# Issuing the first Strassen weight sums of w_bl and w_out one quad earlier in a hybrid decoder layer on Trainium2

## The chip, the core and the metric

The kernel runs on one core of one Trainium2 chip. The metric is device time in microseconds (us), as the median of several runs; the profile is that of one execution, taken by the hardware profiler. The engines go by these names: PE is TensorE's matmul, PEld its weight load, DVE is VectorE, ACT is ScalarE, POOL is GpSimd, and SP issues most of the DMAs. Each engine works through its own queue in order, and semaphores make it wait for the others.

## The reference

One layer on a sequence of 1024 tokens with 1024 channels, in float32. An RMS-normalised input goes through a large projection `w_in`. Its parts feed two branches. The S5 branch (a complex diagonal state-space model) ends in a gated linear unit with `w_glu` and the projection `w_bs`; the RG-LRU branch ends in `w_bl` (1280 x 1024). The two results are merged by gates and multiplied with `w_out` (1024 x 1024). Then come a residual sum and a gated per-layer embedding with `w_ple` and `w_ple_gate`:

```python
z_l = (y_l * jax.nn.silu(lru_g)) @ w_bl[i]
merged = jax.nn.sigmoid(gate_s) * z_s + jax.nn.sigmoid(gate_l) * z_l
x = x + rms_norm(merged @ w_out[i], g_post[i])
x = x + (p[i] @ w_ple[i]) * jax.nn.sigmoid(x @ w_ple_gate[i])
```

## The kernel before

**Arithmetic.** A float32 product is made of three faster ones. Each operand is split into a high part (a rounded copy, type fp32r) and a low part (the rest), and `three` (line 315) issues the matmuls high x high (L317), then high x low and low x high (both L319), each of a 128 x 128 weight block with 128 x 512 data. So the weight's low part is loaded last of the three.

**The weight stream.** `weight_plan` (line 37) lists all weights once, in the order in which PE uses them, as 212 "quads" of up to four blocks of 128 x 128, counted from 0. Class `Weights` walks this list. `load` (L163) issues the DMA of a chunk of eight blocks from HBM into one of four raw buffers; `fetch` decides in the program when a chunk may be loaded. `make` prepares quad after quad in a ring of six buffers: ACT writes the high part (L222). For plain quads of w_bs, w_out and most of w_ple_gate, ACT then writes the negated rounded value into the low part's place (L225), and a DMA that POOL issues adds the raw value to it (L226). For every other quad the low part is "owed", and `lows` has DVE subtract (L234) a little later. `next` hands a quad to the matmuls, and `ahead` is called ahead of each quad:

```python
    def ahead(self, held=1):
        n = self.pos + self.RING - 1 - held
        self.make(n)
        self.lows(n - 1)
        self.fetch(n + 8)
        self.sum(n + 2)
```

Here `pos` is the quad that PE's program uses next, so with `held` at 1 quad `pos + 4` is made and the sums reach to `pos + 6`.

**Strassen pairs.** Part of w_bl's and of w_out's product is done by Strassen's method, which saves one product in eight. Its weights are sums and differences of blocks. Two chunks, a pair, hold A11, A12 and A21, A22. The list then has quads of other kinds than "plain": O2 stands for S2 = A21 + A22 - A11, S1 for A21 + A22, S3 for A11 - A21, S4 and O4 for A12 - S2, A22 for itself. `sum` (line 179) issues these on POOL, one instruction each (all L194): at an O2 quad S1 and S2, in buffers that each pair uses again, and the others at their own quads. At an O2 quad it also calls `lows(i)` (line 204), which has DVE make all low parts owed up to there, since those of the pair before still read the buffers.

**The order around the change.** Quads 112 to 119 are plain quads of w_glu, used alternately by `ps_eb` and `ps_ea` in `brows` (line 1248; 24 matmuls a quad). Quads 120 to 143 are the four pairs of w_bl: O2, S1, a plain quad, S3, S4, A22 each. Quads 144 to 151 are plain quads of w_bs, whose products (`ps_F`) are gated into the merged rows `mg`. Quads 152 to 157 are plain quads of w_out, used in `product` (line 1495; 12 matmuls a quad): 152 to 155 start the banks `oX0` to `oX3`, 156 and 157 add to the first two. Then follow four pairs of w_out, quads 158 to 173, each O2, S3, S1 and S4 or O4, whose products go to `oY`, `oZ`, `oW` and `oV`. After each product `tick` (line 329) runs one step of the data-side work: beside 152 `t_raw(3)` (line 1388), where DVE makes differences of merged rows (L1390, L1391, L1393, L1395) that ACT and DVE split (`lagged`, L1367, and `flush`, L1374), and beside 153 the first of the T1 operand. ACT, DVE, POOL and PE are issued in the order written in the program (`manual_schedule`); SP's order is the scheduler's.

Of the kernel before, what the change touches and what calls it, by code (L numbers as in the profile page):

```python
# [116 lines left out]
BLOCKS, QUADS = weight_plan()  # L117
# [18 lines left out]
class Weights:  # L136
# [42 lines left out]
    def sum(self, upto):  # L179
        G = self.nc.gpsimd  # L180
        while len(self.ready) <= min(upto, len(QUADS) - 1):
            i = len(self.ready)
            self.fetch(i)
            q = QUADS[i]
            s = self.sums
            if q[0] == "O2" and len(self.done) < i:
                return

            def add(name, a, b, op, into=None):
                if into is None:  # L190
                    s[name] = self.tmp.tile([P, HT], F32, tag=name, name=f"w{name}_{i}")
                else:
                    s[name] = s[into]
                G.tensor_tensor(s[name], s[a], s[b], op)  # L194

            if q[0] == "plain":
                _, c, o, n = q
                self.ready.append((self.raws[c][:, o * P:(o + n) * P], n))
                continue
            if q[0] in FIRST:  # L200
                r0, r1 = (self.raws[c] for c in q[1:3])
                s.update(A11=r0[:, :HT], A12=r0[:, HT:], A21=r1[:, :HT], A22=r1[:, HT:])
            if q[0] == "O2":
                self.lows(i)
                add("S1", "A21", "A22", ALU.add)
                add("S2", "S1", "A11", ALU.subtract)
            if q[0] in ("S4", "O4"):
                add("S4", "A12", "S2", ALU.subtract, "S2")
            if q[0] == "S3":
                add("S3", "A11", "A21", ALU.subtract, "A21")  # L210
            self.ready.append((s[q[0].replace("O", "S")], 4))
# [41 lines left out]
def tile_hybrid_trunk(  # L253
# [43 lines left out]
    make_identity(nc, ident)  # L297
    halfpi = cst([P, 1], "halfpi", math.pi / 2)
    cp_t = cst([P, sum(n for _, n in CPAR)], "cp_t")
    sp8 = cst([P, NL], "sp8")  # L300
    nsp8 = cst([P, NL], "nsp8")
# [173 lines left out]
    ple_sb = [two_rows(i, f"ple_sb{i}") for i in (4, 5, 13, 2)]  # L475
    scratch = page(8, "scratch", F32)
    NPAR = sum(n for _, n in SPAR)
    NPT = NPAR - 2048
    pt = scratch[:, :NPT]
# [1218 lines left out]
```

## Time and profile before

| | |
|---|---|
| median of 3 runs | 928.76 us (928.12 to 930.4) |
| profiled execution | 928.25 us, its span 926.5 us |
| mean granted clock of TensorE | 0.999 |
| DMA | 134.21 MB, mean 145 GB/s |

The page of the profile gives for each engine its busy time, share of the span and number of instructions. A view of waits gives, for an engine, the instruction that waited, what released it, and then the total, the number of times and the longest. A timeline gives per row the start, the length, engine, line and operation, what is written from what, and in brackets the idle time before it with its releaser. Times count from the start of the span. `wq` is a quad in the ring, `wraw` a raw chunk, `wS` a sum, `mT` and `mB` operands of w_out's product.

### The profile page before, as it was taken

What the parts mean: (1) busy time and instruction counts of PE and PEld (TensorE: products, weight loads), DVE (VectorE), ACT (ScalarE), POOL (GpSimd) and SP (SyncE); (2) the same over time, 40 slices, a digit from 0 to 9 for tenths busy, and PEclk for the clock granted to TensorE, in tenths of its full rate; (3) what the DMA queues carried; (4) which work ended last, traced back from release to release, by engine and by line L of the source; (5) the groups of instructions that cost most, each with busy time, mean ns of one, the idle gap of its engine ahead of it and who ended that gap; (6) DMA issues with size and microseconds to landing.
All of it is one profiled execution on the core that took longest, in us unless ns stands there. A gap on an engine that the chain in (4) does not pass through costs nothing.

```text
span 926.5 us, 11716 instructions
## 1 busy us (share of the span) xinstructions
PE 919.0 (99%) x4228; PEld 760.3 (82%) x4228; DVE 624.6 (67%) x977; ACT 469.1 (51%) x714; POOL 150.6 (16%) x159
## 2 busy tenths in 40 slices
PE   9999999999999999999999999999999999999997
PEld 7888888888888888888888888888888887887886
DVE  6885566666664347766666767687862798886863
ACT  6643233444443356666666668544534355558531
POOL 1218112212220000000000000022322126422100
PEclk9999999999999999999999999999999999999999
DMA  9745445564533201111111116811479975499951
GB/s 358 277 126 160 126 142 166 172 171 133 173 97 113 74 29 52 52 46 51 52 52 52 47 34 216 291 56 55 141 255 244 247 193 206 119 245 233 301 184 56
DMA packets 70442, 134.21 MB, mean 145 GB/s; under 512 B 18416, under 2 KB 32880, under 8 KB 70384
## 3 DMA queue, kind: packets, MB, share of 16 engines
q1 hardware_dynamic: 64768, 122.72, 41.7%
q0 software_dynamic: 5472, 10.49, 6.3%
q8 instruction: 33, 0.54, 0.2%
q10 hardware_dynamic: 144, 0.26, 0.1%
q14 instruction: 25, 0.20, 0.1%
HBM read 95.30 MB, written 27.53 MB: 133 GB/s over the span
## 4 chain that ended last, share of the span: by engine, by line
PE 89%; issue 6%; DMA 2%; DVE 1%; POOL 1%; ACT 0%; POOLq 0%; SPq 0%
PE ps_L L319 16%; PE ps_L L317 8%; PE ps_rx L319 8%; PE ps_rg L319 8%; PE ps_rg L317 4%; PE ps_rx L317 4%; PE ps_F L319 3%; PE ps_u L319 3%; PE bZ L319 3%; PE ps_pg L319 2%; PE bW L319 2%; PE pg L319 2%; PE bX L319 2%; PE ps_ple L319 2%; PE ps_ea L319 2%
## 5 line engine op out<-in xcount | busy, mean ns | idle before, releaser
L319 PE MATMUL ps_L<-hB,wq 128*128 128x512 f32 x640 | 197.4, 390 | 0.0
L319 PEld LDWEIGHTS ps_L<-hB,wq 128*128 128x128 f32 x640 | 120.3, 188 | 24.3
L317 PE MATMUL ps_L<-hB,wq 128*128 128x512 f32 x320 | 127.1, 397 | 0.0
L222 ACT ACTIVATE wq<-wraw 128x512 fp32r<-128x512 f32 (+1 forms) x188 | 112.5, 613 | 24.1 <-issue 9.2
L234 DVE TENSOR_TENSOR wq<-wraw,wq 128x512 fp32r<-128x512 f32 (+1 forms) x152 | 105.0, 706 | 3.1 <-ACT wq L222 3.1
L319 PE MATMUL ps_rg<-hB,wq 128*128 128x512 f32 x320 | 98.5, 389 | 0.0
L319 PE MATMUL ps_rx<-hB,wq 128*128 128x512 f32 x320 | 98.5, 389 | 0.0
L319 PE MATMUL ps_pg<-x1hl,wq 128*128 128x512 f32 x240 | 74.9, 392 | 0.3 <-DVE x1hl L1374 0.2
L317 PEld LDWEIGHTS ps_L<-hB,wq 128*128 128x128 f32 x320 | 60.2, 188 | 13.3 <-issue 1.7
L319 PEld LDWEIGHTS ps_rg<-hB,wq 128*128 128x128 f32 x320 | 60.1, 188 | 12.5
L319 PEld LDWEIGHTS ps_rx<-hB,wq 128*128 128x128 f32 x320 | 60.1, 188 | 12.4
L194 POOL TENSOR_TENSOR wS<-wraw 128x512 f32<-128x512 f32 x8 | 12.4, 1549 | 354.8 <-DMA wraw<-w_blocks 343.3
L1078 DVE SCALAR_TENSOR_TENSOR c<-ps_rx,cp_t,c 128x1023 f32<-128x1023 f32 (+2 forms) x30 | 38.5, 1282 | 46.2 <-ACT c L1076 45.5
L317 PE MATMUL ps_rx<-hB,wq 128*128 128x512 f32 x160 | 62.3, 389 | 0.0
L317 PE MATMUL ps_rg<-hB,wq 128*128 128x512 f32 x160 | 62.3, 389 | 0.0
L319 PEld LDWEIGHTS ps_pg<-x1hl,wq 128*128 128x128 f32 x240 | 44.8, 188 | 11.5 <-DVE x1hl L1374 1.7
L1015 ACT ACTIVATE sg<-ps_L 128x1024 f32<-128x1024 f32 x20 | 20.5, 1027 | 59.7 <-issue 52.5
L226 POOL DMA_DIRECT2D wq<-wraw x36 | 31.8, 883 | 100.1 <-ACT wq L225 65.6
L317 PE MATMUL ps_pg<-x1hl,wq 128*128 128x512 f32 x120 | 47.0, 391 | 0.0
L319 PE MATMUL ps_u<-hB,wq 128*128 128x512 f32 x128 | 39.8, 392 | 0.4 <-DVE hB L736 0.4
L319 PE MATMUL ps_F<-ys,wq 128*128 128x512 f32 x128 | 39.4, 389 | 0.0
L1086 ACT ACT_TABLE_LOAD x9 | 11.5, 1283 | 51.2 <-DVE yr L1115 51.2
(360 smaller groups left out, 1927.0 us busy)
## 6 DMA issues: line engine op xcount, KB each, us to landing
wraw<-w_blocks SPq DMA_DIRECT2D x95, 512.0 KB
wq<-wraw POOLq DMA_DIRECT2D x36, 256.0 KB, 6.0
xt<-x_t SPq DMA_DIRECT2D x8, 512.0 KB
ple_d<-ple_sb SPq DMA_DIRECT2D x8, 512.0 KB
wn<-sbt SPq DMA_DIRECT2D x8, 512.0 KB
sgl_d<-sg SPq DMA_DIRECT2D x8, 512.0 KB
wn<-pt_d SPq DMA_DIRECT2D x16, 256.0 KB
sgs_d<-sg SPq DMA_DIRECT2D x8, 512.0 KB
```

The lines of the kernel that those rows point to most:

```text
L194: G.tensor_tensor(s[name], s[a], s[b], op)
L222: nc.scalar.activation(hi, src, AF.Copy)
L226: nc.gpsimd.dma_start(lo.bitcast(F32), src, accum_op=ALU.add)
L234: self.nc.vector.tensor_tensor(lo, src, hi.bitcast(F32), ALU.subtract)
L317: T.matmul(ps, wh, xh, start=start, stop=False, skip_group_check=more)
L319: T.matmul(ps, a, b, start=False, stop=stop and a is (wh if xl_last else wl), skip_group_check=more)
L1015: S.activation(t, ps, AF.Sigmoid)
L1078: V.scalar_tensor_tensor(c[:, d:], ps[:, :NT - d], w_[3 - d], c[:, d:], ALU.mult, ALU.add)
L1086: S.activation(sq, ps, AF.Sigmoid)
```

## The change

In `sum`, the test that holds back the sums of an O2 quad is replaced. Before, they waited until every quad ahead of it was made. Now they are held back only while their chunk's load has not been issued in the program, or while a quad that is not plain is still unmade ahead.

```diff
             q = QUADS[i]
             s = self.sums
-            if q[0] == "O2" and len(self.done) < i:
+            if q[0] == "O2" and (q[1] not in self.raws or any(QUADS[j][0] != "plain" for j in range(len(self.done), i))):
                 return
```

`self.done` is the list of made quads and `self.raws` holds the chunks whose loads were issued. What is summed, by which instructions and into which buffers stays as it was.

## The prediction

> **What bounds the kernel now.** I read the page's busy times first, then the waits of PE (the matmul engine) and of its weight loads.
>
> ```profile
> PE 919.0 (99%) x4228; PEld 760.3 (82%) x4228; DVE 624.6 (67%) x977; ACT 469.1 (51%) x714; POOL 150.6 (16%) x159
> ...
> PE warm L500 <- DVE halfpi L291: 1.1, 1, 1.1
> PE ps_ple L317 <- DVE p_hi L526: 0.8, 1, 0.8
> PE ps_u L319 <- DVE hB L736: 0.4, 1, 0.4
> PE oY L319 <- DVE wq L234: 0.3, 1, 0.3
> PE ps_pg L319 <- DVE x1hl L1374: 0.2, 1, 0.2
> ...
> PEld oY L319 <- DVE wq L234: 1.0, 2, 0.7
> ```
>
> PE is busy 919.0 of 926.5 us, and all its named waits come to 2.8 us. Only one has to do with Strassen weight sums: `oY`, the product that uses the O2 quad of w_out, waits for a low part. No product of w_bl is in either list. So little can be gained, and only in the w_out stage. The timeline of PE there, around that wait:
>
> ```profile
> 768.39 0.39 PE L317 MATMUL oY<-mT,wq 128*128 128x512 f32 x1
> ...
> 769.29 0.50 PE L319 MATMUL oY<-mT,wq 128*128 128x512 f32 x1 [0.29 <-DVE wq L234]
> ...
> 771.69 0.39 PE L317 MATMUL oZ<-mT,wq 128*128 128x512 f32 x1
> ...
> 774.41 0.39 PE L317 MATMUL oW<-mT,wq 128*128 128x512 f32 x1
> ```
>
> A quad is 12 matmuls. Undisturbed it takes 774.41 - 771.69 = 2.72 us; this one took 771.69 - 768.39 = 3.30. The wait costs **0.58 us**, and that is the largest gain there is.
>
> **What moves.** In the planned order quads 112 to 119 (w_glu) and 144 to 157 (w_bs, then plain w_out) are plain; O2 of the first pair is quad 120 for w_bl and 158 for w_out. The old test issues its sums when all earlier quads are made, in the call of `ahead` that makes quad 119 or 157. The new test lets them out in the call before, since `sum` looks two quads past the last one made and the one still unmade is plain. Later pairs have A22, S4 or O4 ahead of them, so their test comes out as before. No instruction is added; S1 and S2 move up one quad, and S3 stays where it is.
>
> POOL's timeline shows what its queue holds at the two places (L226 issues the DMA that completes a low part, L194 is a sum), and SP's one load before each:
>
> ```profile
> 603.96 1.30 POOL L194 TENSOR_TENSOR wS<-wraw 128x512 f32<-128x512 f32 x1 [335.77 <-DMA wraw<-w_blocks]
> ...
> 758.01 0.86 POOL L226 DMA_DIRECT2D wq<-wraw  x1 [6.32 <-ACT wq L225]
> 761.87 0.86 POOL L226 DMA_DIRECT2D wq<-wraw  x1 [3.00 <-ACT wq L225]
> 762.43 1.61 POOL L194 TENSOR_TENSOR wS<-wraw 128x512 f32<-128x512 f32 x1
> 764.12 1.63 POOL L194 TENSOR_TENSOR wS<-wS,wraw 128x512 f32<-128x512 f32 x1
> 765.71 1.74 POOL L194 TENSOR_TENSOR wraw<-wraw,wraw 128x512 f32<-128x512 f32 x1
> ...
> 597.25 0.43 SPq L163 DMA_DIRECT2D wraw<-w_blocks  x1
> ...
> 747.23 0.33 SPq L163 DMA_DIRECT2D wraw<-w_blocks  x1
> ```
>
> **The w_bl pair: nothing.** POOL stood idle for 335.77 us ahead of S1 and was released by a load's landing. Its queue was empty, so an earlier place in the program cannot start the sum earlier. What does change is DVE's order: `lows(i)` at line 204 now flushes the low part of quad 118 one call earlier, and no longer takes that of quad 119 with it, which goes out one call later.
>
> ```profile
> 609.55 0.67 DVE L234 TENSOR_TENSOR wq<-wraw,wq 128x512 fp32r<-128x512 f32 x1
> ...
> 614.72 1.29 DVE L234 TENSOR_TENSOR wq<-wraw,wq 128x512 fp32r<-128x512 f32 x2
> ...
> 632.39 0.39 PE L317 MATMUL ps_ea<-geo,wq 128*128 128x512 f32 x1
> ```
>
> At 609.55 is quad 117, at 614.72 are 118 and 119. One moves to 610.2 and delays what follows by 0.6 us; the other moves a quad of 24 matmuls, 5.4 us, to about 621. PE first needs quad 119 at 632.39, so 11 us cover it. Cost 0; if DVE were 11 us behind there, it would cost what exceeds that.
>
> **The w_out pair: sums ahead of the DMA of quad 157.** The queue was DMA(156), DMA(157), S1, S2, S3; it becomes DMA(156), S1, S2, DMA(157), S3. From a DMA's issue to the next sum POOL takes 762.43 - 761.87 = 0.56 us, so S1 can start at 758.01 + 0.56 = **758.57**. Its raw data were loaded from 747.23; the load at 597.25 took until 603.96, 6.7 us, so I put this landing at 753.9, in time. S1 and S2 take 765.71 - 762.43 = 3.28 us and end at 761.85, when DMA(157) went out before. In the queue alone nothing is lost. But DVE and ACT are not idle in those 3.3 us. ACT's timeline, then DVE's, then DVE's two instructions under the old sums as a group:
>
> ```profile
> 759.30 0.63 ACT L1367 ACTIVATE mT<-mtmp 128x512 fp32r<-128x512 f32 x1 [1.10 <-DVE mtmp L1391]
> 759.90 0.63 ACT L1367 ACTIVATE mT<-mg 128x512 fp32r<-128x512 f32 x1
> 760.44 0.61 ACT L222 ACTIVATE wq<-wraw 128x512 fp32r<-128x512 f32 x1
> 760.96 0.62 ACT L225 ACTIVATE wq<-wraw 128x512 fp32r<-128x512 f32 x1
> ...
> 761.96 1.14 ACT L1367 ACTIVATE mT<-mg 128x512 fp32r<-128x512 f32 x2
> ...
> 765.79 0.63 ACT L222 ACTIVATE wq<-wS 128x512 fp32r<-128x512 f32 x1 [2.69 <-POOL wS L194]
> ...
> 758.57 0.69 DVE L1391 TENSOR_TENSOR mtmp<-mg,mg 128x512 f32<-128x512 f32 x1
> 759.18 0.69 DVE L1393 TENSOR_TENSOR mg<-mg,mg 128x512 f32<-128x512 f32 x1
> ...
> 762.61 1.99 DVE L1374 TENSOR_TENSOR mT<-mg,mT 128x512 fp32r<-128x512 f32 x1 [0.75 <-ACT mT L1367]
> ...
> L1374 DVE TENSOR_TENSOR mT<-mg,mT 128x512 fp32r<-128x512 f32 x2 | 3.7, 1883 | 0.8 <-ACT mT L1367 0.8
> ```
>
> A DVE tensor_tensor takes 0.69 us alone and 1.88 (mean of two) while POOL sums. The moved sums fall on `t_raw(3)`: L1391 starts at 758.57, the very time S1 can start, and L1393 behind it. ACT's splits at 759.30 and 759.90 wait for these two, and behind them in ACT's queue stand both halves of quad 157 (760.44, 760.96), for whose end DMA(157) waits. So a stretch on DVE passes through ACT and POOL to the low part of quad 157. How late that may be, from PE's weight loads and from what the landing view gives for DMA(157) and for DMA(156):
>
> ```profile
> 765.45 0.19 PEld L317 LDWEIGHTS oX<-mB,wq 128*128 128x128 f32 x1
> 765.67 0.41 PEld L319 LDWEIGHTS oX<-mB,wq 128*128 128x128 f32 x2
> ...
> DMA to landing us min/median/max: 3.2/3.2/3.2
> ...
> DMA to landing us min/median/max: 3.7/3.7/3.7
> ```
>
> Quad 157 starts 2.72 us before 768.39, at 765.67; its first low part is the second of the two loads listed at 765.67, at about 765.90. The DMA landed at 761.87 + 3.2 = 765.07: slack 0.83, or 0.33 with the other landing time. Two ends for the stretch. If DVE gets L1391 in first, only L1393 is stretched, by 1.88 - 0.69 = 1.19 us: PE waits 1.19 - 0.83 = 0.36 to 1.19 - 0.33 = 0.86. If S1 is first, both are, by 1.99 - 0.69 + 1.19 = 2.49: PE waits 1.66 to 2.16. I take the first: DVE runs without a gap there and has L1391 at hand, while S1 still has to follow a DMA issue. Middle 0.61.
>
> In return S2 is done at about 762.4 instead of 765.75. ACT no longer stands 2.69 us before 765.79, and the low part of quad 158 is no longer late: even with quad 157 delayed, hi(158) follows the two T1 splits of 761.96, at 761.96 + 1.19 + 1.14 = 764.3. That gives back the 0.58. Next in line would be DVE's backlog, which PE's delay covers.
>
> On who waits, the Trainium skill, in "SBUF — State Buffer", section "Who interferes with whom", says that a DVE instruction with two SBUF inputs contends with a GpSimd instruction that reads SBUF, and that whoever issues first holds the shared ports for the whole instruction. The instruction at 762.61 agrees: it ended 0.56 us after S1 (762.43 + 1.61). By the group's mean both DVE instructions would be stretched whoever comes first, and PE would wait 2.38 - 0.83 = 1.55 to 2.38 - 0.33 = 2.05 us; by the rule the first of a tie goes free, which is the lower end I took.
>
> **The sum**, on the profiled execution (928.25 us, of which the span is 926.5): -0.58 + 0.61 = +0.03, so 928.28; bounds -0.58 + 0.36 = -0.22 to -0.58 + 2.16 = +1.58. The median of the runs, 928.76, is 0.51 above the profiled execution, so I add that: **928.8**.
>
> **Rivals.**
> - *Clean gain*: the sums slip into POOL's pause and DVE's stretch stays under the slack. For: POOL had 3.00 us idle before 761.87. Against: L1391 and L1393 lie exactly there. Gain 0.58: 928.2.
> - *POOL wins the tie*: both DVE instructions are stretched and PE waits about 1.9 at quad 157, net +1.33: 930.1. For: at 762.61 it was DVE that was held. It decides from the point where S1 starts before 758.57.
> - *The sum waits for its raw load* and holds DMA(157) behind it on POOL. Every us that the load lands after 758.57 passes to PE once the slack is gone: net = landing + 3.28 + 3.2 - 765.90 - 0.58 = landing - 760.0. To be slower by 0.3% (2.8 us) the landing must be after 762.8, 15.6 us from issue against 6.7, or the load issued 9 us later. SP's queue is ordered by the scheduler, not by hand, so I don't exclude it: 931.6 or more.
> - *Nothing moves*: S1 doesn't start earlier at w_out either, as at w_bl. 928.8 again. Against: POOL's releaser at 761.87 is ACT, not a load.
>
> **The numbers.** Forecast 0.42; POOL wins 0.23; clean gain 0.2; nothing moves 0.1; late load 0.05. A measurement of this kernel can tell about 0.3%, 2.8 us, from no change; all but the last stay inside. The runs before spread over 2.3 us, so the range is 928.2 and 930.1 with half that spread, 1.1, on either side: 927.1 to 931.2. Faster by more than 0.3% has no case, only scatter, 0.03; slower has the last case and scatter, 0.07; same 0.90.
>
> **What would show it.** S1 near 758.6 to 759.2 ahead of the last L226 on POOL; L1393 stretched to some 1.9 us; that last L226 at 763 or later and a wait of 0.4 to 0.9 us of `oX` on the DMA shortly after 765.7; `oY` with no wait on L234, its quad in 2.72 us; S1 of w_bl still released by a load at about 604. It is wrong if any stage but w_out changes by over 1 us, or if quad 157 loses nothing while `oY` still waits.

## The result, and the profile after

The changed kernel takes 929.22 us (median of 22 runs, 928.93 to 933.01) against 928.26 us (22 runs, 927.82 to 930.4): a ratio of 1.0013, 95% interval 1.0007 to 1.0019. By the interval that is 0.6 to 1.8 us slower (the medians lie 0.96 us apart), less than the 0.3% named in the prediction, and its interval lies clear of 1. The profiled execution took 929.39 us, its span 927.6 us, 1.1 more than before.

The page's busy times and the waits of PE and its weight loads, after:

```profile
PE 918.9 (99%) x4228; PEld 760.3 (82%) x4228; DVE 626.0 (67%) x977; ACT 469.1 (51%) x714; POOL 150.3 (16%) x159
...
PE oX L319 <- DMA wq<-wraw: 1.4, 1, 1.4
...
PEld oX L319 <- DMA wq<-wraw: 1.9, 1, 1.9
```

The wait of `oY` on L234 has left the list, and a larger one has come: `oX`, on the DMA that completes a low part. PE's timeline shows where, and what it costs:

```profile
765.78 0.39 PE L317 MATMUL oX<-mB,wq 128*128 128x512 f32 x1
766.01 0.39 PE L319 MATMUL oX<-mB,wq 128*128 128x512 f32 x1
767.83 0.50 PE L319 MATMUL oX<-mB,wq 128*128 128x512 f32 x1 [1.43 <-DMA wq<-wraw]
...
770.24 0.39 PE L317 MATMUL oY<-mT,wq 128*128 128x512 f32 x1
...
772.96 0.39 PE L317 MATMUL oZ<-mT,wq 128*128 128x512 f32 x1
```

Quad 157 now takes 770.24 - 765.78 = 4.46 us, 1.74 more than an undisturbed quad; the named wait is 1.43 of this. Quad 158 behind it takes 772.96 - 770.24 = 2.72: its 0.58 is won. The chain behind the loss, read upward from the DMA: POOL's timeline, then DVE's, then ACT's.

```profile
604.81 1.68 POOL L194 TENSOR_TENSOR wS<-wraw 128x512 f32<-128x512 f32 x1 [336.52 <-DMA wraw<-w_blocks]
...
758.13 0.86 POOL L226 DMA_DIRECT2D wq<-wraw  x1 [6.32 <-ACT wq L225]
758.69 1.61 POOL L194 TENSOR_TENSOR wS<-wraw 128x512 f32<-128x512 f32 x1
760.38 1.64 POOL L194 TENSOR_TENSOR wS<-wS,wraw 128x512 f32<-128x512 f32 x1
764.56 0.86 POOL L226 DMA_DIRECT2D wq<-wraw  x1 [2.55 <-ACT wq L225]
...
758.68 2.17 DVE L1391 TENSOR_TENSOR mtmp<-mg,mg 128x512 f32<-128x512 f32 x1
760.78 1.77 DVE L1393 TENSOR_TENSOR mg<-mg,mg 128x512 f32<-128x512 f32 x1
...
760.89 0.63 ACT L1367 ACTIVATE mT<-mtmp 128x512 fp32r<-128x512 f32 x1 [2.58 <-DVE mtmp L1391]
762.59 0.63 ACT L1367 ACTIVATE mT<-mg 128x512 fp32r<-128x512 f32 x1 [1.07 <-DVE mg L1393]
763.13 0.62 ACT L222 ACTIVATE wq<-wraw 128x512 fp32r<-128x512 f32 x1
763.65 0.62 ACT L225 ACTIVATE wq<-wraw 128x512 fp32r<-128x512 f32 x1
```

S1 starts 0.56 us behind the DMA issue at 758.13, and both DVE instructions of `t_raw(3)` are held, not one. L1391 ends at 760.85, 0.55 after S1 (760.30). ACT's splits wait for the two, the halves of quad 157 stand behind the splits, and the last DMA goes out at 764.56, 2.69 later than before (0.11 of this comes from an earlier stage). POOL was free from 762.02 and waited 2.55 us for ACT. At w_bl, the first row, S1 is still released by a load.

The span's 1.1 us adds up from PE's timelines: 0.11 us before the w_out products (these start at 752.18 instead of 752.07), 1.74 lost at quad 157, 0.58 won at 158, and 0.13 won at the `oY` of the second pair: 0.11 + 1.74 - 0.58 - 0.13 = 1.14.

### The profile page after: what moved, and what is told of

It is laid out like the page before. It is cut to its first block, busy times and chain, and to the rows that moved or that the text cites. A ratio compares the mean times of both kernels' runs of the same rounds, so it can differ in the third digit from the quotient of the medians.

```text
span 927.6 us, 11719 instructions
## 1 busy us (share of the span) xinstructions
PE 918.9 (99%) x4228; PEld 760.3 (82%) x4228; DVE 626.0 (67%) x977; ACT 469.1 (51%) x714; POOL 150.3 (16%) x159
## 4 chain that ended last, share of the span: by engine, by line
PE 88%; issue 6%; DVE 2%; DMA 2%; POOL 1%; ACT 0%; POOLq 0%; DVEq 0%; ACTq 0%
PE ps_L L319 16%; PE ps_L L317 8%; PE ps_rg L319 8%; PE ps_rx L319 8%; PE ps_rg L317 4%; PE ps_rx L317 4%; PE ps_u L319 3%; PE bZ L319 3%; PE ps_F L319 3%; PE ps_pg L319 2%; PE bW L319 2%; PE bX L319 2%; PE pg L319 2%; PE ps_ple L319 2%; PE ps_ea L319 2%
## 5 line engine op out<-in xcount | busy, mean ns | idle before, releaser
L234 DVE TENSOR_TENSOR wq<-wraw,wq 128x512 fp32r<-128x512 f32 (+1 forms) x152 | 105.2, 708 | 3.2 <-ACT wq L222 3.1
```

The costliest lines, as they stand in the source:

```text
L234: self.nc.vector.tensor_tensor(lo, src, hi.bitcast(F32), ALU.subtract)
```

## The experiments

All eight were timed in five rounds, 11 runs each against 33 of the kernel before on the same chip; a profile shows one of the 11. The stretch theory: the moved sums hold up DVE, DVE holds up ACT, and ACT the DMA of quad 157. The rivals: POOL's queue order by itself, or the work at w_bl. Line numbers shift with the lines that an experiment adds; the operations tell which is which.

**Which pair.** The test was changed for one pair at a time.

```diff
-            if q[0] == "O2" and len(self.done) < i:
+            if q[0] == "O2" and len(self.done) < i - (i == 158):    # wout_only
+            if q[0] == "O2" and len(self.done) < i - (i == 120):    # wbl_only
```

> The earlier issue for quad 158 (w_out) alone, w_bl's first pair as before. Stretch theory (the moved sums S1 and S2 stretch DVE's two instructions of t_raw(3), ACT's halves of quad 157 wait for those, and PE waits for that quad's low part): all of the loss is here, ratio 1.0011 to 1.0013, a wait of oX on a DMA of 1.4 us. Rival (the loss comes from DVE's changed order at w_bl or from SP's order that the scheduler changed): a ratio within 0.0005 of 1.

> The earlier issue for quad 120 (w_bl) alone, w_out's first pair as before. Stretch theory: POOL's first sum is released by its load as before, DVE's changed order is covered, ratio 1.0000 within 0.0004, oY's wait of 0.3 us is still there. Rival (the loss comes from w_bl): ratio 1.0010 or more.

`wout_only` gave 1.0011 (1.0003 to 1.002), `wbl_only` 0.9998 (0.9989 to 1.0007). From `wbl_only`: POOL's first sum, DVE's low parts of w_glu's last quads, and the old wait in PE's list.

```profile
604.03 1.30 POOL L194 TENSOR_TENSOR wS<-wraw 128x512 f32<-128x512 f32 x1 [336.07 <-DMA wraw<-w_blocks]
...
609.62 1.28 DVE L234 TENSOR_TENSOR wq<-wraw,wq 128x512 fp32r<-128x512 f32 x2
620.06 0.70 DVE L234 TENSOR_TENSOR wq<-wraw,wq 128x512 fp32r<-128x512 f32 x1
...
PE oY L319 <- DVE wq L234: 0.2, 1, 0.2
```

Low part 118 has joined 117 at 609.62, 119 has gone to 620.06, both as worked out, and nothing waits for them. The loss is all at w_out.

The profile of `wout_only` is that of the slowest of its 11 runs (931.69 us, median 929.2), and in it `oX` waits 1.9 us on the DMA instead of the expected 1.4. A row of DVE's timeline well ahead of the place shows why:

```profile
725.88 0.69 DVE L1423 TENSOR_TENSOR mg<-mg,msr 128x512 f32<-128x512 f32 x1 [0.82 <-DMA msr<-ms_d]
```

DVE had waited 0.82 us for a load of `msr`, rows that it adds to `mg`; the profiles of the kernel before and of the changed kernel have no such wait. DVE hardly stops between there and `t_raw(3)`, so L1391 starts 7.29 us behind PE's first `oX` matmul instead of 6.50. The profiles of `dve_first`, `two_earlier` and `after_l1391` have the same late load (1.15, 0.57 + 0.44 and 0.29 us), so their waits can't be laid to the sums alone.

**Queue or DVE.** Quad 157 is made one call earlier, so ACT's halves stand ahead of `t_raw(3)`'s splits. In `quad157_first` its DMA goes ahead of the sums too; in `halves_first` the DMA stays behind S1 and S2, as in the changed kernel.

```diff
+        product(xs[p_], "B11", True, keep, 0 if p_ == 0 else 1)   # both: W.ahead(0) at quad 152
...
+                if i == 157:                                      # halves_first, in make
+                    self.rest = (lo.bitcast(F32), src)
...
+                if i == 158:                                      # halves_first, in sum, behind S2
+                    G.dma_start(*self.rest, accum_op=ALU.add)
```

> The kernel before, with quad 157 made one call earlier (ahead with held at 0 at quad 152), so that ACT's two halves of it stand ahead of t_raw(3)'s splits and its DMA ahead of the sums; S1, S2 and S3 follow it on POOL near 759.5, about as early as in the changed kernel. Stretch theory: DVE is stretched just as much, but nothing of quad 157 waits for DVE any more, and the low part of quad 158 is in time: no wait of oX, none of oY, 0.6 to 0.7 us faster than before, ratio 0.9992 to 0.9994. Rival (early sums cost PE through another way, T2 and T3 operands for instance): oY or oZ waits, ratio 1.0000 or more.

> S1 and S2 of quad 158 stand on POOL between DMA(156) and DMA(157), as in the changed kernel, but ACT's two halves of quad 157 are made ahead of t_raw(3)'s splits, so only POOL's queue and no longer DVE stands before DMA(157). Stretch theory (DVE, then ACT, then the DMA): L1391 and L1393 are as long as in the changed kernel (2.2 and 1.8 us), yet DMA(157) goes out near 761.8 as in the kernel before, no wait of oX, none of oY, ratio 0.9990 to 0.9994. Rival (POOL's queue, the sums ahead of DMA(157), makes it late): oX waits 1 us or more, ratio 1.0005 or more.

`quad157_first` gave 0.999 (0.9981 to 0.9999), `halves_first` 0.9992 (0.9983 to 1.0001). POOL's and DVE's timelines of `halves_first`:

```profile
758.12 1.62 POOL L194 TENSOR_TENSOR wS<-wraw 128x512 f32<-128x512 f32 x1
759.81 1.63 POOL L194 TENSOR_TENSOR wS<-wS,wraw 128x512 f32<-128x512 f32 x1
761.39 0.85 POOL L208 DMA_DIRECT2D wq<-wraw  x1
...
758.12 2.17 DVE L1396 TENSOR_TENSOR mtmp<-mg,mg 128x512 f32<-128x512 f32 x1
760.22 1.78 DVE L1398 TENSOR_TENSOR mg<-mg,mg 128x512 f32<-128x512 f32 x1
```

DVE is held as long as in the changed kernel, the sums stand ahead of the DMA as there, and PE waits for neither `oX` nor `oY`. So the place behind the two sums costs nothing here; it is ACT's place behind DVE that makes the DMA late. `quad157_first` is faster than both kernels: its median is 927.43 us against 928.28 of the kernel before beside it. Its first `oY` quad runs from 768.25 to 770.97, 2.72 us.

**How much of the sums.** `half_early` does 256 of the 512 columns of S1 and S2 at the new place and the rest behind DMA(157).

```diff
+                n = 256 if i == 158 and name in ("S1", "S2") else HT
+                G.tensor_tensor(s[name][:, :n], s[a][:, :n], s[b][:, :n], op)
...
+            if i == 159:
+                s1, s2, a11, a21, a22 = (t[:, 256:] for t in self.rest)
+                G.tensor_tensor(s1, a21, a22, ALU.add)
+                G.tensor_tensor(s2, s1, a11, ALU.subtract)
```

> The changed kernel with S1 and S2 of quad 158 cut in two by columns: 256 of 512 at the new place, the other 256 behind DMA(157), ahead of S3; the result is the same. Stretch theory: the two DVE instructions are held for sums half as long, about 1.5 us in total instead of 2.6, DMA(157) goes out near 763.4, PE waits 0.5 to 0.9 us at quad 157 and oY does not wait or hardly, ratio 0.9998 to 1.0004. Rival (a fixed cost per sum or per change of order, whatever its length): oX waits 1.4 us or more, ratio 1.0010 or more.

It gave 1.0003 (0.9994 to 1.0012). DVE's timeline, POOL's DMA(157) and PE's wait:

```profile
758.48 1.63 DVE L1398 TENSOR_TENSOR mtmp<-mg,mg 128x512 f32<-128x512 f32 x1
760.04 1.23 DVE L1400 TENSOR_TENSOR mg<-mg,mg 128x512 f32<-128x512 f32 x1
...
763.27 0.87 POOL L233 DMA_DIRECT2D wq<-wraw  x1 [2.56 <-PE oX L326]
...
PE oX L326 <- DMA wq<-wraw: 0.3, 1, 0.3
```

The two DVE instructions grow by 0.94 + 0.54 = 1.48 us over 0.69 each, instead of 2.56 in the changed kernel. The profile names PE as what released DMA(157), but ACT's second half of quad 157 ended at 762.97, 0.30 us ahead of it, as in the changed kernel. The six `oX` quads end 0.64 us late (from 751.98 to 768.94, against 6 x 2.72), instead of 1.74. S2 is complete no earlier than before, so `oY` waits a little again, and the balance is about even. The cost falls with the length of the sums: without half of the columns, 1.08 of the 2.56 us are gone.

**Who goes first.** The prediction had let L1391 go free. Two attempts to bring that about: a POOL memset ahead of S1 (`dve_first`), and S1 issued inside `t_raw(3)`, made to wait for L1391 (`after_l1391`, where `W.early` lifts the old test).

```diff
+                if i == 158:                                      # dve_first
+                    G.memset(self.tmp.tile([P, HT], F32, tag="S2", name="gap")[:, :256], 0.0)
...
+        if k == 3:                                                # after_l1391, behind L1391
+            G.tensor_copy(W.tmp.tile([P, HT], F32, tag="S2", name="gap")[:, :1], t[:, :1])
+            W.early = True
+            W.sum(158)
```

> The changed kernel with one POOL memset of 128 x 256 put ahead of S1 of quad 158, which adds about 0.3 us of POOL time, so that L1391 is already running on DVE when S1 asks for memory. Stretch theory with the first of the two going free: L1391 back to about 0.7 us, only L1393 stretched, S1 held by 0.3 us instead; the last plain DMA of w_out on POOL goes out near 763.2 instead of 764.6, PE waits 0.2 to 0.9 us at quad 157, ratio 0.9997 to 1.0003. Rival (both are stretched whoever comes first, by the mean of 1.88): PE waits 1.4 us or more, ratio 1.0010 to 1.0015. Rival (POOL's queue itself delays DMA(157)): 0.3 us later than in the changed kernel, ratio 1.0015.

> S1 and S2 of quad 158 are issued inside t_raw(3), behind a POOL copy of one column that reads what L1391 wrote, so that S1 cannot start before L1391 is done: the case that the prediction took. Theory as predicted (only L1393 can be stretched): L1391 is 0.7 us, PE waits 0.3 to 0.9 us at quad 157, partly because DMA(157) now also stands behind S2 on POOL until about 763, oY doesn't wait, ratio 0.9997 to 1.0003. Rival (the cost is that of two sums on DVE's queue however they fall): PE waits 1.4 us or more, ratio 1.0008 or more.

`dve_first` missed: 1.0016 (1.0007 to 1.0025). Its late load, its POOL and DVE timelines and PE's wait:

```profile
725.81 0.69 DVE L1425 TENSOR_TENSOR mg<-mg,msr 128x512 f32<-128x512 f32 x1 [1.15 <-DMA msr<-ms_d]
...
759.26 0.65 POOL L206 MEMSET gap<- 128x256 f32 x1
759.53 1.62 POOL L194 TENSOR_TENSOR wS<-wraw 128x512 f32<-128x512 f32 x1
...
759.28 2.43 DVE L1393 TENSOR_TENSOR mtmp<-mg,mg 128x512 f32<-128x512 f32 x1
761.63 1.78 DVE L1395 TENSOR_TENSOR mg<-mg,mg 128x512 f32<-128x512 f32 x1
...
PE oX L321 <- DMA wq<-wraw: 2.3, 1, 2.3
```

The difference (L1393 in this file) started 0.25 us ahead of S1 and was still held until 0.56 us after S1's end (761.15). But POOL's memset is recorded 0.02 us ahead of the difference, so this run didn't put DVE clearly first. The longer wait is mostly the load's: the difference starts 7.63 us behind PE's first `oX` matmul instead of 6.50, while the two held instructions together take 4.13 us instead of 3.87. `after_l1391` gave 0.9995 (0.9986 to 1.0004), with DVE's two, then S1 and DMA(157):

```profile
758.89 0.69 DVE L1392 TENSOR_TENSOR mtmp<-mg,mg 128x512 f32<-128x512 f32 x1
759.50 0.68 DVE L1398 TENSOR_TENSOR mg<-mg,mg 128x512 f32<-128x512 f32 x1
...
760.19 1.28 POOL L195 TENSOR_TENSOR wS<-wraw 128x512 f32<-128x512 f32 x1
...
763.12 0.86 POOL L227 DMA_DIRECT2D wq<-wraw  x1
```

Here S1 came so late (760.19) that neither was held. DMA(157) went out 1.25 us later against PE than in the kernel before, by its place behind S2 and by 0.32 us of the late load. The `oX` quads end 0.42 us late (they run from 752.07 to 768.81): 0.31 is lost at quad 156, whose DMA took 5.2 us to land instead of 3.7, and 0.11 at quad 157. So the predicted 0.3 to 0.9 at quad 157 didn't come, and L1393 wasn't held; the case in which L1391 goes free and a held L1393 makes DMA(157) late was not reached by any run.

**Earlier still.** `two_earlier` issues S1 and S2 two calls ahead of the old place, on POOL before DMA(156).

```diff
+            if q[0] == "O2" and len(self.done) < i - 2 * (i == 158):
...
+        self.sum(n + 3 if n + 3 == 158 else n + 2)
```

> The sums of quad 158 two calls earlier than before, on POOL ahead of DMA(156) instead of DMA(157). Stretch theory with DVE as a full queue (it has no gap from 740 to 762 in the kernel before): whatever DVE work the sums meet, all behind it is late by about 2.5 us, L1391 and L1393 too, though these are 0.7 us long again; oX waits 1.2 to 2 us in total, at quad 156 or 157, ratio 1.0005 to 1.0015. Rival (only the meeting with L1391 and L1393 counts): no wait of oX, none of oY, ratio 0.9990 to 0.9994.

It gave 1.0015 (1.0006 to 1.0023). DVE's timeline has the differences of `t_raw(2)`, which the sums now meet, and those of `t_raw(3)`; then PE's wait:

```profile
752.68 2.17 DVE L1391 TENSOR_TENSOR mtmp<-mg,mg 128x512 f32<-128x512 f32 x1
754.77 1.79 DVE L1393 TENSOR_TENSOR mg<-mg,mg 128x512 f32<-128x512 f32 x1
...
762.25 0.69 DVE L1391 TENSOR_TENSOR mtmp<-mg,mg 128x512 f32<-128x512 f32 x1
762.86 0.68 DVE L1393 TENSOR_TENSOR mg<-mg,mg 128x512 f32<-128x512 f32 x1
...
PE oX L319 <- DMA wq<-wraw: 2.4, 1, 2.4
```

`t_raw(3)` is unstretched but 3.7 us later than before, because DVE's queue was full from 752 on. Of this, 1.29 us were there ahead of the sums (L1390 of `t_raw(2)` at 751.96 instead of 750.67; 0.34 of it is from an earlier stage, the rest from late loads of `msr`), and about 2.4 come from the sums. PE waits already at quad 156. The wait is longer than the expected 1.2 to 2 us in total; this profile is that of the slowest of the 11 runs (932.28 us, median 929.27). Going earlier doesn't avoid the cost as long as ACT stands behind a full DVE.

## Why the prediction was right or wrong

- **w_bl: nothing.** Right. `wbl_only` is level, S1 waits for the same load, and the two low parts moved to where they were put.
- **The gain of 0.58 at quad 158.** Right, and in every profile in which `oY` had no wait its quad took 2.72 us (2.77 under the lowered clock of `wout_only`). The second pair's 0.13 us was left out of the sum.
- **The path DVE, ACT, DMA(157), PE.** Right; `halves_first` shows that without ACT's step the held DVE costs nothing. The slack of 0.83 was right too, since DMA(157) took 3.2 us to land in these profiles as before. Counted from PE's first `oX` matmul, it went out later than in the kernel before by 2.58 us in the changed kernel, 1.49 in `half_early`, 1.25 in `after_l1391` and 3.97 in `dve_first`. The six `oX` quads lost 1.74, 0.64, 0.42 and 3.13 us, which is each of these less 0.83, to within 0.02.
- **Which of the two is held.** Wrong: the step that took the lower end, "DVE runs without a gap there and has L1391 at hand". In the changed kernel S1 held the one and S2 the other, for 2.17 and 1.77 us, and PE lost 1.74 instead of 0.61. That lies in the range of the rival *POOL wins the tie* (1.66 to 2.16), and also in that of the reading by the group's mean, both stretched whoever comes first (1.55 to 2.05); the runs don't tell these two apart. The net is -0.58 - 0.13 + 1.74 = +1.03.
- **The rule beside it.** The Trainium skill, "SBUF — State Buffer", section "Who interferes with whom", lets whoever issues first hold the shared ports. That the loser is held to the other's end agrees (0.55 us after S1's end here). Who is first can't be read off the recorded starts: an instruction on DVE that started 0.43 us ahead of S1 lost in `quad157_first` (last section).
- **From the profile to the median.** The 0.51 added for it came from three runs; with 22, the median before is 928.26, level with the profiled 928.25. So 928.8 stood 0.5 too high by this and 1.0 too low by the step above, and that the measured 929.22 lies near it is partly luck, since the two errors cancel. The range was wide enough for every rival but the late load, so that the time lies in it says little for the mechanism.
- **SP's order.** The scheduler moved one load of x behind two weight loads; no wait shows it.

## What to carry to other kernels

Ahead of moving work earlier on one engine, look at what the other engines do at the new place and not only at its own queue: here POOL had 3 us free, and using them held up DVE. A copy that a DMA waits for shouldn't stand in an engine's queue behind work that depends on a full neighbour; putting it one step ahead turned a loss of 0.13% into a gain of 0.1%. And a tie between two engines for one resource is no ground for taking the cheaper end.

## What the runs showed of the hardware

**TensorE's clock can halve after a wait of about 2 us.** In the profiled execution of `wout_only` (span 929.9 us) PE stood idle for 1.91 us at quad 157. PE's timeline, then the windows view around it (window, length, busy us and instructions of PE, PEld, DVE, ACT, POOL, granted clock, DMA share, GB/s):

```profile
768.50 0.55 PE L319 MATMUL oX<-mB,wq 128*128 128x512 f32 x1 [1.91 <-DMA wq<-wraw]
...
769.28 1.05 PE L319 MATMUL oX<-mB,wq 128*128 128x512 f32 x2
...
768.00:769.00 1.00, 0.49 (x2) 0.44 (x3) 1.00 (x2) 1.00 (x3) 0.00 (x0) 0.91 0.01 0
769.00:770.00 1.00, 1.00 (x4) 0.81 (x3) 1.00 (x3) 1.00 (x3) 0.07 (x1) 0.50 0.19 29
...
772.00:773.00 1.00, 1.00 (x6) 0.77 (x5) 1.00 (x3) 1.00 (x3) 0.00 (x0) 0.89 1.09 299
```

The clock fell to 0.50 just behind the wait and came back after about 3.4 us (from 768.8 to 772.2, by the shares of the first and last windows), two matmuls taking 1.05 us instead of 0.62. From the end of the wait to the first `oY` matmul PE took 3.99 us (768.50 to 772.49), against 2.41 in the changed kernel (767.83 to 770.24), so the drop cost 1.58 us beside the wait. This span is 2.3 us above the changed kernel's. `two_earlier`'s profile has the same drop after 2.41 us; `dve_first`, idle for 2.3 us, has none. The Trainium skill, "TensorE: Matmul & The Clock Gate", Part 1, describes a free-running window of about 3.4 us; the length agrees, and these runs add that the drop can follow a wait shorter than such a window. The changed kernel's runs reach up to 933.01 us and those of `quad157_first` only to 927.86. Whether the drop makes this tail is not shown: the run of 933.01 has a mean granted clock of 0.998, but those of 930.35 to 930.71 have 0.999 to 1.0, and one of 929.19 has 0.997. What the profiles do show is that a late load of `msr` passes through DVE, ACT and DMA(157) to PE once the slack of 0.83 is used up, and the moved sums use it up.

**What holds DVE.** POOL's timeline of `quad157_first`, then DVE's:

```profile
758.92 0.86 POOL L226 DMA_DIRECT2D wq<-wraw  x1 [0.18 <-issue]
759.48 1.61 POOL L194 TENSOR_TENSOR wS<-wraw 128x512 f32<-128x512 f32 x1
...
759.05 2.60 DVE L1393 TENSOR_TENSOR mg<-mg,mg 128x512 f32<-128x512 f32 x1
```

A DVE instruction that had started 0.43 us ahead of S1 by the records was held until 0.56 us after S1's end (761.09), and here too S1 came straight behind a DMA issue on POOL. The record of this issue runs to 759.78, past S1's start, so starts on POOL are recorded roughly. It can come out the other way: in the kernel before, a sum at 769.38 had been waiting for DVE, and the DVE instruction that had started 0.23 us ahead of it (L234 at 769.15) took its 0.69 us. What sets who waits stays open.
